# Three projections of a hybrid layer moved from one stage's fill to the next, and small and dense matrix products in a fixed turn

## The chip, the cores and the metric

The kernel runs on one core of one Trainium2 chip. The core has a matrix engine (TensorE, "PE" in the rows, with its weight loads as "PEld"), VectorE ("DVE"), ScalarE ("ACT"), GpSimd ("POOL") and SyncE ("SP"), whose queue issues the transfers. Each engine works through its own instructions in a fixed order and waits on semaphores for the others. The metric is the device time of one execution in microseconds, the median of several runs.

## What is computed

The reference is one inference step of two trunk layers. Each layer takes 384 tokens of width 1024 (128 of context, 256 latent), as a feed-forward half step, a mixer, and another feed-forward half step. The mixer is what matters here:

```python
def merge_branches(oa, ob, oc, zg, lp):
    ga, gb, gc = jnp.split(jax.nn.sigmoid(zg), 3, axis=-1)
    merged = ga * (oa @ lp['proj_a']) + gb * (ob @ lp['proj_b']) + gc * (oc @ lp['proj_c'])
    return merged @ lp['w_out']
```

`oa` and `ob` come from two kinds of attention with 8 heads each, `oc` from a recurrence with 8 heads of 64 that runs once in each direction, from projections r, k and v of the layer's input that pass a convolution over three tokens:

```python
def step(S, inp):
    r_t, w_t, k_t, v_t, kk_t, a_t = inp
    sa = jnp.einsum('bhvk,bhk->bhv', S, -kk_t)
    S = S * w_t[:, :, None, :] + sa[..., None] * (kk_t * a_t)[:, :, None, :] + v_t[..., None] * k_t[:, :, None, :]
    return S, jnp.einsum('bhvk,bhk->bhv', S, r_t)
```

## The kernel before

**Dense products.** All weights come as 128 x 128 blocks in one stream of 512 KB units of 8 blocks (`Stream`, line 370). Each unit is split by ScalarE into a rounded half `hi` and by VectorE into the rest, `lo` (both recorded at line 291, as nearly all instructions of these two engines). A chunk is one block times one slice of the input: three matmuls (lines 401, 402 and 403 in `mm3_steps`) of 128 x 128 by 384 columns. `mm3_steps` traces two chunks at a time, a block of 6 matmuls, and then yields a cost of 0.96 us (0.48 per chunk). A projection with its convolution is `conv_gen`: 8 chunks into the tile `pc`, an eviction by ScalarE and four VectorE instructions, and for a k the head norms (`kss`). Gates are written from `pz`, output projections from `pp`.

**The attention and its fill.** `attention` runs 8 pairs of heads through `heads_pair`, a chain of products (`sc`, `sl`), softmax on VectorE and ScalarE, transposes (`pt`) and output products (`po`). Between the steps of that chain it puts dense work from `front_fill`, which follows the plan `XP`: one string for each slot, in which g is a gate, n the next projection that the attention needs, p an output projection, and c the next projection for the recurrence out of the list `C_FIRST`. A slot spreads its string evenly over the steps of its pair. Dense work of a slot is put behind the attention's last matmul, so it does not run ahead of it.

**The recurrent stage.** `rwkv_gen` goes through four pairs of heads. For each, `rwkv_prepare` makes the inputs, `rwkv_chunks` turns the recurrence into products over chunks of 64 tokens, and `rwkv_scan` carries the state over. Pair 0's preparation comes first. After that the chunks of a pair are interleaved with the preparation of the next pair (`front`) and the scan of the pair before (`back`). In `rwkv_chunks` a long run of VectorE instructions ends in the tile `yr`; then come four groups of the smallest products, 48, 48, 24 and 24 calls of 16 or 32 rows by 32 weight columns, into the tile `pz` at line 1367 (the gates' `pz` stands at lines 401 to 403). Each call appears as two matmuls in the rows.

**What sets the order.** Matmuls of the recurrence go through `rmm`. After each, `beside` adds to a debt of dense work, in proportion to the product's size and to a rate (`RATES` by phase, `FR` outside), and takes blocks out of `mixer_fill` while the debt is positive. Yields of the generators add to the debt too: `RP` for each step of pair 0's preparation, `LAT` by phase, `RA` and `RS`. A scheduler then fixes the order of each engine with its own model of times, by priority. Each dense block is put behind the last product of the recurrence that was traced before it; nothing puts a product of the recurrence behind a dense block.

Of the kernel before, what the change touches and what calls it, by code (L numbers as in the profile page):

```python
# [32 lines left out]
OA = 50  # L33
SB = range(0,20)
SF = range(0,8,2)
FR = 0.3
PHASE = [0] * 4 + [1] * 3 + [2] * 4 + [3] * 10
RATES = (0.4, 0.2, 0.8, 0.3)
LAT = (0.2, 0.2, 0.0, 0.4)
RS = 2  # L40
RP = 7
OC = 100
PIL = 3
GAPS = (2, 1, 2, 0)
# [13 lines left out]
AHD = (4,)  # L58
HV = (3,)
AB = 6  # L60
XP = ('gggggg','nc','nggc','nc','nnnc','nnnpppppppp','nnn','nnnc','cc','c')
WY = (0.5, 0.5, 0.5, 1.5, 1, 1.5, 1, 1)
SCB = 2
LATE = 1
XS = 4
P3V = 0
PNV = 0
A0 = 4
A1 = 16
C_FIRST = ["tw", "al", "k0", "r0", "v0", "k1", "r1", "v1"]  # L70
CH = 64
NCH = NTOK // CH
NCC, NCL = NCTX // CH, NLAT // CH
# [223 lines left out]
def trunk(tc, I, O, order, taps=None, stop=None):  # L297
    nc = tc.nc
    PS = bass.MemoryType.PSUM
    es = ExitStack()  # L300
    V, S, G, T = Engine(nc.vector), Engine(nc.scalar), Engine(nc.gpsimd), nc.tensor
# [87 lines left out]
    def mm3(out, chunks, xs):  # L389

        n = len(chunks)
        for k, (w, x) in enumerate(zip(chunks, xs)):
            block3(out, w, x, k == 0, k == n - 1)

    def mm3_steps(out, chunks, xs, step=2):

        n = len(chunks)
        for k0 in range(0, n, step):
            for k in range(k0, min(n, k0 + step)):
                (wh, wl), (xh, xl) = chunks[k], xs[k]  # L400
                T.matmul(out, wh, xh, start=(k == 0), stop=False)  # L401
                T.matmul(out, wh, xl, start=False, stop=False)  # L402
                T.matmul(out, wl, xh, start=False, stop=(k == n - 1))  # L403
            if k < n - 1:
                yield 0.48 * step

# [6 lines left out]
    cc = cpool.tile([P, KD, 2], F32, name="cc")  # L413
# [18 lines left out]
    def vcol(l, name):  # L432
        o, n = VEC[name]
        return vecs[l][:, o : o + n]
# [500 lines left out]
    def gate_tile(keep):  # L935
        return keep.tile([P, NTOK], F32, tag="gate", bufs=2, name="gt")
# [14 lines left out]
    def front_fill(l, keep, pool, w, oa, need, head):  # L951

        conv = conv_gen(l, keep, pool, w, C_FIRST)
        todo = {"g": (1, (gate(l, 0, i, ax[i], head) for i in range(KD))), "p": (0.5, (project(l, "proj_a", i, ax[i], oa) for i in range(KD)))}
# [10 lines left out]

        for plan in XP:
            yield sum(todo[x][0] if x in todo else 1 for x in plan), some(plan)
# [6 lines left out]
    def mixer_fill(l, keep, pool, w, ob, gcd):  # L974

        for m in range(KD):
            if m == 0:
                yield from conv_gen(l, keep, pool, w, ["gl"])
            elif m in (2, 4):
                yield from conv_gen(l, keep, pool, w, [f"{n}{m // 2 + 1}" for n in "krv"])  # L980
            th = gate_tile(keep)
            yield from gate(l, 1, m, th)
            yield from project(l, "proj_b", m, th, ob)
        for m in range(KD):
            yield from gate_c(l, keep, m, gcd)
# [133 lines left out]
    def attention(l, pool, keep, w, oa, ob, head, spill):  # L1119
# [35 lines left out]
        debt = 0.0  # L1155
        for _ in range(XS):
            step(rest)
# [36 lines left out]
    def branch_a(l, pool, ready, soon, head):  # L1194
# [16 lines left out]
        nc.sync.dma_start(out=O["o_ka"][l], in_=kx[:, :NCTX])  # L1211
        soon.append([LATE, keys])
        yield 0.0
        yield from to_sbuf(l, A_V0, "pv", vx, head)
        nc.sync.dma_start(out=O["o_va"][l], in_=vx[:, :NCTX])
        soon.append([LATE, lambda: vt.append(token_major(pool, vx, "vt"))])
        yield 0.0
# [5 lines left out]
        for m in range(4):  # L1223
# [7 lines left out]

            soon.append([LATE, queries])
            yield 0.0

    def branch_b(l, pool, ready, soon):
# [3 lines left out]
        for m in range(4):  # L1239
# [26 lines left out]
            vt = []  # L1266
            soon.append([LATE, lambda vt=vt, vx=vx: vt.append(token_major(pool, vx, "vt"))])
            yield 0.96
# [16 lines left out]
    def conv_gen(l, keep, pool, w, names):  # L1285

        wsh = vcol(l, "w_shift")
        late = []
        for nm in names:
            i = C_INDEX[nm]  # L1290
            pz = mmp("pc")
            for n, cost in enumerate(mm3_steps(pz[:, :NTOK], stream.take("w_in", l, C_ORDER[i], KD), hs)):
                if n == 1 and late:
                    late.pop()()
                yield cost
            o = keep.tile([P, NTOK], F32, tag=("r" if nm[0] == "r" else nm), bufs=(2 if nm[0] == "r" else 1), name=nm)
            S.activation(out=o, in_=pz[:, :NTOK], func=AF.Copy, scale=wsh[:, 3 * i + 1 : 3 * i + 2])
            for a, b in STREAMS:
                V.scalar_tensor_tensor(out=o[:, a + 1 : b], in0=pz[:, a : b - 1], scalar=wsh[:, 3 * i : 3 * i + 1], in1=o[:, a + 1 : b], op0=ALU.mult, op1=ALU.add)
                V.scalar_tensor_tensor(out=o[:, a : b - 1], in0=pz[:, a + 1 : b], scalar=wsh[:, 3 * i + 2 : 3 * i + 3], in1=o[:, a : b - 1], op0=ALU.mult, op1=ALU.add)  # L1300
            w[nm] = o
            if nm == "tw":
                S.activation(out=o, in_=o, func=AF.Tanh)
            elif nm == "gl":
                S.activation(out=o, in_=o, func=AF.Tanh, scale=0.5)
                V.tensor_scalar(out=o, in0=o, scalar1=0.5, scalar2=0.5, op0=ALU.mult, op1=ALU.add)
            elif nm[0] == "k":

                p = int(nm[1])
                sq = gate_tile(keep)  # L1310
                S.activation(out=sq, in_=o, func=AF.Square, scale=vcol(l, "k_k")[:, p : p + 1])

                def norms(p=p, sq=sq):
                    pss = mmp("kss")
                    head_sums(pss, sq)
                    w[f"rn{p}"] = rn = keep.tile([P, 6], F32, name=f"rn{p}")
                    S.activation(out=rn, in_=pss[:, 0:6], func=AF.Sqrt)
                    V.tensor_scalar(out=rn, in0=rn, scalar1=1e-12, scalar2=None, op0=ALU.max)
                    V.reciprocal(rn, rn)

                late.append(norms)
            elif nm == "al":
                ka = keep.tile([P, 2, 4], F32, name="ka2")
                V.tensor_scalar(out=ka[:, 0], in0=vcol(l, "k_a"), scalar1=0.5, scalar2=None, op0=ALU.mult)
                V.tensor_scalar(out=ka[:, 1], in0=vcol(l, "k_a"), scalar1=-0.5, scalar2=1.0, op0=ALU.mult, op1=ALU.add)
                w["ka"] = ka
                hb = keep.tile([P, 2, 8], F32, name="hb")
                V.tensor_scalar(out=hb[:, 0], in0=vcol(l, "decay_w0"), scalar1=0.5, scalar2=None, op0=ALU.mult)
                V.tensor_scalar(out=hb[:, 1], in0=vcol(l, "iclr_a0"), scalar1=0.5, scalar2=None, op0=ALU.mult)
                w["hb"] = hb  # L1330
            yield 0.96
            yield 0.0
# [18 lines left out]
    rw_last = [None]  # L1351

    dense = [None, 0.0]
    rate = [FR]

# [8 lines left out]
            dense[1] -= b  # L1364

    def rmm(out, lhs, rhs, **k):
        rw_last[0] = T.matmul(out, lhs, rhs, **k)
        beside(lhs.shape[0], int(np.prod(lhs.shape[1:])), int(np.prod(rhs.shape[1:])))

    def rtr(out, src):  # L1370
# [27 lines left out]
    def rwkv_gen(l, pool, keep, w, oc, add):  # L1398
        gt = pool.tile([P, 2 * NU + 4, 3 * CH], F32, name="gt")

        end = gt[:, 2 * NU :].rearrange("p u x -> p (u x)")
        V.memset(end, 0.0)
        V.memset(end[:, 0:256:17], 1.0)
        t16 = end[:, 0:256].rearrange("p (a b) -> p a b", b=16)
        z1 = end[:, 256 : 256 + 32 * NU].rearrange("p (u t) -> p u t", t=32)
        fix = (gt, end, t16, z1)
        xs = [{} for _ in range(4)]
        for cost in rwkv_prepare(l, 0, w, pool, xs[0]):
            yield RP * cost
        for p in range(4):  # L1410
            back = ahead(rwkv_scan(l, p - 1, w, pool, keep, oc, xs[p - 1]), OC) if p else iter(())
            front = ahead(rwkv_prepare(l, p + 1, w, pool, xs[p + 1]), OA) if p < 3 else iter(())
            rate[0] = RATES[0]
            for i, cost in enumerate(ahead(rwkv_chunks(l, p, w, pool, fix, xs[p]), OB)):
                rate[0] = RATES[PHASE[i + 1]]
                yield LAT[PHASE[i]] * cost
                if i == 0:
                    add(0, f"v{min(p + 1, 3)}")
                if i in SB:
                    yield RA * next(back, 0)  # L1420
                if i in SF:
                    yield RA * next(front, 0)
            rate[0] = FR
            for b in chain(back, front):
                yield RA * b
        dense[1] = 0.0
        for cost in ahead(rwkv_scan(l, 3, w, pool, keep, oc, xs[3]), 500):
            yield RS * cost
# [326 lines left out]
    with es:  # L1755
        with tc.tile_pool(name="init", bufs=1) as pool:
# [15 lines left out]
            for c0 in range(0, KD, 2):  # L1772

                offset = 9000 - 1000 * c0
                i, cols = c0 // 4, slice(256 * (c0 % 4), 256 * (c0 % 4) + 512)
                pa = rwp("ada")
                for k in range(0, KD, 2):
                    w = pool.tile([P, 2, 512], F32, tag="adaw", bufs=KD, name="adaw")
# [60 lines left out]
```

## Time and profile before

| what | value |
| --- | --- |
| runs | 2411.74, 2412.66, 2422.63 us; median 2412.66 |
| profiled execution | 2413.25 us, span 2411.4 us, mean granted clock 0.985 |
| instructions in the span | 42684 |
| TensorE busy | 2289.0 us |
| VectorE busy | 1689.8 us |
| ScalarE busy | 1066.2 us |
| GpSimd busy | 409.2 us |

The span runs from the first to the last instruction. Matmuls overlap in the engine, so the distance between two starts, and not a matmul's own duration, tells what it takes. A wait in the timeline is given in brackets behind the instruction that it precedes, with what ended it.

### The profile page before, as it was taken

How to read it: one execution, taken by the hardware profiler on the slowest of the kernel's cores; microseconds unless marked ns; L12 is line 12 of the kernel's file. 1: busy time of each engine (PE TensorE's matmuls, PEld its weight loads, DVE VectorE, ACT ScalarE, POOL GpSimd, SP SyncE). 2: the span in 40 equal slices, each digit the busy share in tenths (PEclk: the TensorE clock that was granted, in tenths of full speed). 3: DMA queues.
4: the chain of work that ended last, by engine and by line, in shares of the span. 5: the costliest groups of instructions: out<-in, count | busy, mean ns of one | idle time of the engine just before them, and what ended most of it. 6: DMA issues, size and time to landing. Idle time of an engine off the chain costs nothing.

```text
span 2411.4 us, 42684 instructions
## 1 busy us (share of the span) xinstructions
PE 2289.0 (95%) x17066; PEld 2098.1 (87%) x17066; DVE 1689.8 (70%) x2949; ACT 1066.2 (44%) x1962; POOL 409.2 (17%) x426
## 2 busy tenths in 40 slices
PE   8999899998899999999899999999989999999998
PEld 6999888887777788999889999888877777899997
DVE  3896877767767567876879964767787674775534
ACT  3333245655545445433243332556555454453322
POOL 1000421001122034000430003300022220530003
PEclk9999999999899999999999999999999999999999
DMA  8775544242111262665546733533321112634332
GB/s 307 246 244 184 184 115 124 90 116 71 37 61 48 72 212 88 218 205 178 168 148 218 246 127 126 153 95 93 112 71 33 55 54 81 216 122 132 123 125 85
DMA packets 125078, 324.53 MB, mean 135 GB/s; under 512 B 31568, under 2 KB 50256, under 8 KB 124880
## 3 DMA queue, kind: packets, MB, share of 16 engines
q1 hardware_dynamic: 124880, 321.81, 41.6%
q8 instruction: 134, 2.20, 0.4%
q14 instruction: 64, 0.52, 0.1%
HBM read 312.06 MB, written 9.70 MB: 133 GB/s over the span
## 4 chain that ended last, share of the span: by engine, by line
PE 74%; DVE 12%; ACT 5%; issue 3%; POOL 3%; DMA 1%; SPq 0%; ACTq 0%; POOLq 0%; DVEq 0%
PE po L403 5%; PE po L402 5%; PE po L401 5%; PE pa L385 4%; PE pa L386 4%; PE pg L385 4%; PE pg L386 4%; PE pa L387 4%; PE pg L387 4%; DVE lo L291 3%; ACT hi L291 2%; PE pz L401 2%; PE pz L402 2%; PE pz L403 2%; POOL ax L291 1%
## 5 line engine op out<-in xcount | busy, mean ns | idle before, releaser
L291 ACT ACTIVATE hi<-raw 128x1024 fp32r<-128x1024 f32 x418 | 441.7, 1058 | 743.1 <-issue 227.1
L291 DVE TENSOR_TENSOR lo<-raw,hi 128x1024 fp32r<-128x1024 f32 (+1 forms) x472 | 551.4, 1177 | 303.3 <-ACT hi L291 301.0
L291 DVE SCALAR_TENSOR_TENSOR acc<-adaw,cs,acc 128x1024 f32<-128x1024 f32 x224 | 289.0, 1330 | 0.0
L403 PE MATMUL po<-uh,lo 128*128 128x384 f32 x704 | 238.3, 338 | 10.7 <-DVE lo L291 10.5
L401 PE MATMUL po<-uh,hi 128*128 128x384 f32 x704 | 238.7, 339 | 0.0
L402 PE MATMUL po<-ul,hi 128*128 128x384 f32 x704 | 237.5, 337 | 0.0
L385 PE MATMUL pa<-zh,hi 128*128 128x384 f32 x584 | 198.7, 340 | 0.0
L386 PE MATMUL pa<-zl,hi 128*128 128x384 f32 x584 | 197.4, 338 | 0.0
L385 PE MATMUL pg<-zh,hi 128*128 128x384 f32 x584 | 197.2, 338 | 0.0
L387 PE MATMUL pa<-zh,lo 128*128 128x384 f32 x584 | 196.3, 336 | 0.6 <-DVE lo L291 0.6
L386 PE MATMUL pg<-zl,hi 128*128 128x384 f32 x584 | 196.6, 337 | 0.0
L387 PE MATMUL pg<-zh,lo 128*128 128x384 f32 x584 | 196.2, 336 | 0.0
L291 POOL TENSOR_TENSOR sa<-ax,ax 128x384 f32<-128x384 f32 x12 | 15.8, 1312 | 788.8 <-DVE ax L291 585.2
L403 PEld LDWEIGHTS po<-uh,lo 128*128 128x128 f32 x704 | 133.2, 189 | 13.2 <-DVE lo L291 13.2
L401 PE MATMUL pz<-zh,hi 128*128 128x384 f32 x352 | 127.0, 361 | 8.3 <-ACT hi L291 2.8
L401 PEld LDWEIGHTS po<-uh,hi 128*128 128x128 f32 x704 | 133.0, 189 | 2.1 <-issue 1.5
L402 PEld LDWEIGHTS po<-ul,hi 128*128 128x128 f32 x704 | 133.0, 189 | 0.5
L403 PE MATMUL pz<-zh,lo 128*128 128x384 f32 x352 | 124.8, 355 | 2.2 <-DVE lo L291 2.2
L402 PE MATMUL pz<-zl,hi 128*128 128x384 f32 x352 | 123.8, 352 | 0.0
L385 PEld LDWEIGHTS pa<-zh,hi 128*128 128x128 f32 x584 | 109.6, 188 | 4.9 <-ACT hi L291 3.7
L387 PEld LDWEIGHTS pa<-zh,lo 128*128 128x128 f32 x584 | 110.1, 189 | 0.9 <-DVE lo L291 0.9
L387 PEld LDWEIGHTS pg<-zh,lo 128*128 128x128 f32 x584 | 110.1, 189 | 0.0
(398 smaller groups left out, 5323.5 us busy)
## 6 DMA issues: line engine op xcount, KB each, us to landing
raw<-ws SPq DMA_DIRECT2D x418, 512.0 KB, 3.5
adaw<-wada SPq DMA_DIRECT2D x144, 512.0 KB, 4.5
bm<-rpb SPq DMA_DIRECT2D x64, 64.0 KB, 7.9
axd<-ax SPq DMA_DIRECT2D x16, 192.0 KB, 4.2
gcd<-gt SPq DMA_DIRECT2D x16, 192.0 KB, 4.6
gc<-gcd SPq DMA_DIRECT2D x16, 192.0 KB, 3.4
ax<-axd SPq DMA_DIRECT2D x16, 192.0 KB, 4.7
xt<-xt SPq DMA_DIRECT2D x8, 192.0 KB, 8.4
```

The costliest lines, as they stand in the source:

```text
L291: self.last = f(*a, **k)
L385: T.matmul(out, wh, xh, start=first, stop=False)
L386: T.matmul(out, wh, xl, start=False, stop=False)
L387: return T.matmul(out, wl, xh, start=False, stop=last)
L401: T.matmul(out, wh, xh, start=(k == 0), stop=False)
L402: T.matmul(out, wh, xl, start=False, stop=False)
L403: T.matmul(out, wl, xh, start=False, stop=(k == n - 1))
```

## The change

The list of projections in the attention's fill ends after those of pair 0. k1, r1 and v1 are taken at the start of the recurrent stage's fill, ahead of `gl`. The plan of the attention's slots has one c less in its third, seventh and eighth slot (the first string fills the time before the loop). The rates of the debt change, the preparation's factor goes from 7 to 5, and 2 us are added once, for pair 0, at the yield in front of the smallest products. `mm3_steps` notes the last matmul of each block in `filled`; `rmm` puts a product with up to 32 weight columns behind that matmul, when there was a block since the last product of the recurrence.

```diff
-FR = 0.3
+FR = 0.35
 PHASE = [0] * 4 + [1] * 3 + [2] * 4 + [3] * 10
-RATES = (0.4, 0.2, 0.8, 0.3)
+RATES = (0.5, 0.25, 0.7, 0.35)
...
-RP = 7
+RP = 5
...
-XP = ('gggggg','nc','nggc','nc','nnnc','nnnpppppppp','nnn','nnnc','cc','c')
+XP = ('gggggg','nc','nggc','n','nnnc','nnnpppppppp','nnn','nnn','c','c')
...
+FIRST = 2
...
-C_FIRST = ["tw", "al", "k0", "r0", "v0", "k1", "r1", "v1"]
+C_FIRST = ["tw", "al", "k0", "r0", "v0"]
...
+    filled = [None]
+
     def mm3_steps(out, chunks, xs, step=2):
...
                 T.matmul(out, wh, xl, start=False, stop=False)
-                T.matmul(out, wl, xh, start=False, stop=(k == n - 1))
+                filled[0] = T.matmul(out, wl, xh, start=False, stop=(k == n - 1))
...
             if m == 0:
-                yield from conv_gen(l, keep, pool, w, ["gl"])
+                yield from conv_gen(l, keep, pool, w, ["k1", "r1", "v1", "gl"])
...
     def rmm(out, lhs, rhs, **k):
-        rw_last[0] = T.matmul(out, lhs, rhs, **k)
+        small = int(np.prod(lhs.shape[1:])) <= 32
+
+        with tc.issue_after(filled[0].ins) if small and filled[0] is not None else ExitStack():
+            rw_last[0] = T.matmul(out, lhs, rhs, **k)
+        filled[0] = None
         beside(lhs.shape[0], int(np.prod(lhs.shape[1:])), int(np.prod(rhs.shape[1:])))
...
-                yield LAT[PHASE[i]] * cost
+
+                yield LAT[PHASE[i]] * cost + (FIRST if p == 0 and i == 6 else 0)
```

## Rows read from the trace of the kernel before

**Rows 1.** The page, busy time, share and instructions of the engines.

```profile
PE 2289.0 (95%) x17066; PEld 2098.1 (87%) x17066; DVE 1689.8 (70%) x2949; ACT 1066.2 (44%) x1962; POOL 409.2 (17%) x426
```

**Rows 2.** Busy time by stretch: attention, recurrent stage, first layer, then second.

```profile
core 0: us, PE busy (x) PEld busy (x) DVE busy (x) ACT busy (x) POOL busy (x), PEclk, DMA share, GB/s
378.00:563.50 185.50, 179.82 (x1058) 160.49 (x1060) 127.81 (x336) 108.86 (x272) 3.10 (x3) 0.99 0.33 96
563.50:862.50 299.00, 277.05 (x3483) 227.64 (x3479) 207.14 (x435) 148.10 (x275) 60.30 (x90) 0.97 0.18 58
1570.00:1756.70 186.70, 179.60 (x1060) 160.26 (x1062) 129.02 (x339) 110.23 (x276) 3.09 (x3) 0.99 0.33 97
1756.70:2051.00 294.30, 272.31 (x3481) 224.37 (x3477) 207.62 (x435) 148.05 (x276) 61.05 (x90) 0.98 0.19 59
```

**Rows 3.** Timeline of TensorE at the joints between pairs of the attention.

```profile
436.98 0.45 PE L1069 MATMUL sl<-kh,qs 128*128 128x384 f32 x1 [0.66 <-ACT pe L291]
...
518.64 0.86 PE L1097 MATMUL po<-ptl,vt 128*64 128x256 f32 x5 [1.38 <-ACT ptl L291]
...
539.89 0.44 PE L401 MATMUL pc<-zh,hi 128*128 128x384 f32 x1
...
560.78 0.65 PE L1097 MATMUL po<-ptl,vt 128*64 128x256 f32 x2 [1.82 <-ACT ptl L291]
...
562.87 1.54 PE L1097 MATMUL po<-ptl,vt 128*64 128x256 f32 x5 [0.64 <-ACT ptl L291]
```

**Rows 4.** Timeline of TensorE around the first pair's smallest products.

```profile
611.05 0.34 PE L402 MATMUL pc<-zl,hi 128*128 128x384 f32 x1
611.23 0.33 PE L403 MATMUL pc<-zh,lo 128*128 128x384 f32 x1
...
614.62 0.98 PE L1367 MATMUL pz<-yr,gt 16*32 16x16 f32 x96 [2.41 <-DVE yr L291]
615.53 0.44 PE L401 MATMUL pc<-zh,hi 128*128 128x384 f32 x1
615.81 0.34 PE L402 MATMUL pc<-zl,hi 128*128 128x384 f32 x1
...
620.24 0.52 PE L403 MATMUL pc<-zh,lo 128*128 128x384 f32 x1
620.56 0.52 PE L401 MATMUL pc<-zh,hi 128*128 128x384 f32 x1
```

**Rows 5.** Waits of TensorE by releaser in 563.5 to 862.5: total, times, longest.

```profile
PE pz L1367 <- DVE yr L291: 3.0, 2, 2.4
...
PE pz L403 <- DVE lo L291: 1.1, 1, 1.1
...
PE pp L401 <- ACT hi L291: 0.6, 1, 0.6
```

**Rows 6.** VectorE: two groups of the attention; then busy times of the run-up.

```profile
L291 DVE TENSOR_TENSOR lo<-raw,hi 128x1024 fp32r<-128x1024 f32 (+1 forms) x30 | 35.6, 1188 | 25.2 <-ACT hi L291 25.1
...
L291 DVE SCALAR_TENSOR_TENSOR k<-pc,vec,k 128x127 f32<-128x127 f32 (+1 forms) x8 | 3.2, 407 | 0.0
...
563.50:614.60 51.10, 45.15 (x293) 37.69 (x290) 42.87 (x77) 24.46 (x44) 13.06 (x22) 0.98 0.20 64
```

**Rows 7.** Line 402 alone, a third of all dense matmuls, in two stretches.

```profile
563.50:614.60 51.10, 17.15 (x50) 9.47 (x50) 0.98 0.20 64
614.60:628.00 13.40, 3.28 (x6) 1.76 (x6) 0.62 0.13 44
```

**Rows 8.** Three stretches at a lower clock; of the second, tile `pc` alone.

```profile
614.60:628.00 13.40, 12.97 (x304) 11.00 (x306) 7.77 (x19) 5.82 (x10) 0.00 (x0) 0.62 0.13 44
1808.00:1816.00 8.00, 3.61 (x11) 2.47 (x10) 0.41 (x1) 0.00 (x0) 0.57 0.02 5
748.00:754.00 6.00, 5.09 (x27) 4.66 (x28) 4.11 (x7) 2.17 (x5) 1.66 (x3) 0.72 0.25 90
```

## The prediction

> **What bounds the kernel now.** I read the page first: TensorE is busy for 95% of the span [rows 1], so work that is only moved from one place to another on this engine can gain nothing but TensorE's waits, a lower clock, or the cost of changing between kinds of product. Then I cut the span into the two stages that the change touches, in both layers [rows 2]. The attention, with its fill, takes 185.5 us in the first layer and 186.7 in the second, and TensorE waits for 5.7 and 7.1 us of them: it is bound by TensorE. The recurrent stage takes 299.0 and 294.3 us with 22.0 us of waits in each, and its mean granted clock is 0.97 and 0.98. What there is to gain lies in the second stage: some 22 us per layer of waits, and stretches at half clock. The last two views say where. The timeline of TensorE [rows 3, 4] shows the waits between the attention's pairs and in front of the smallest products; the waits by releaser [rows 5] show that none but those for `yr` (3.0 us), the input of the first group of smallest products, is large.
>
> **Part 1: 24 chunks leave the attention.** k1, r1 and v1 are three projections of 8 chunks, 3 matmuls each: 72 matmuls. Dense ones start 0.175 us apart in a run (611.05, 611.23) [rows 4], so TensorE loses 72 x 0.175 = 12.6 us of work per layer here. The attention's chain of pairs does not get shorter by itself, so waits appear where the removed projection was the cover. Slots lose one projection each: the third ("nc" to "n"), the seventh ("nnnc" to "nnn") and the eighth ("cc" to "c"). The trace has both forms of the joint: after a slot "nnn" TensorE waits 1.38 us at 518.64, after the slot "nnnc" a `pc` matmul starts at 539.89 with no wait [rows 3]. I add 1.4 us each for the third and the seventh (the third waits 0.66 us already, at 436.98), and 0.5 us for the tail, whose 1.82 and 0.64 us of waits [rows 3] stand behind a chain that also loses the convolutions' work on VectorE. That is 3.3 us of new waits; the bounds are none, and the whole 12.6 us (each slot as long as before). Attention: -12.6 + 3.3 = -9.3 us per layer.
>
> **Part 2: they come into the recurrent stage.** +12.6 us of TensorE work per layer. With them move 3 weight transfers of 512 KB; DMA stands at 0.18 there against 0.33 in the attention [rows 2], so these are hidden behind the stage, on SP's queue too. On VectorE move 12 convolution steps of 0.41 us and 3 `lo` halves of 1.19 us [rows 6], 8.5 us, and on ScalarE the 3 `hi` halves and evictions; ScalarE is busy for half of the stage [rows 2] and hides them.
>
> **Part 3: the run-up to the first small product.** From 563.5 to 614.6 the first pair's chain goes through VectorE, which is busy for 42.9 of 51.1 us [rows 6], and TensorE waits 51.1 - 45.15 = 5.95 us, the 2.41 us before the first small product included [rows 4, 6]. 50 matmuls of each of the three dense kinds, 150 in all, ran by then [rows 7]. More had been released, but it stood behind the small products in TensorE's fixed order. Now the first small product has to come after all dense work released before it. By the constants that is 4 x 5 us in the preparation, some 8 us more in the chunks and 2 us of FIRST: 30 us at 0.48 per chunk, 62 chunks or 186 matmuls, to which the attention's leftover of 12 comes in either version. So 186 + 12 - 150 = 48 more matmuls run before that point: 8.4 us. VectorE gets the 8.5 us of part 2 in the same run-up and has 8.2 us free; I take half of it as added to the chain, 4.2 us. Then the waits are 5.95 + 4.2 - 8.4 = 1.7 us: 4.2 us gained. Bounds: nothing (VectorE's work all lengthens the chain) and 5.95. The gain is real only if the work done early is not missing as cover later. At the end of the stage the dense work still stands between the last scan's steps, and by the constants some 14 chunks stay for it: enough, I take it.
>
> **Part 4: turns.** The 144 calls of the smallest products per pair cost 0.055 x 0.7 each: 5.5 us of dense work, six blocks of 6 matmuls. The added edge names what is queued: the small product behind a block waits for its last matmul, and everything of the recurrence behind that small product waits too, ScalarE's eviction of the group after it. If the block's weights are late, the recurrence is late; that is a rival below. What changing costs: from the small products at 614.62 into dense work the first dense matmul takes 0.28 us to the next one's start (615.53 to 615.81), 0.105 more than in a run [rows 4]; with the same on the way out, 0.2 us a turn. Four of the six blocks fall between groups, where dense matmuls stand already; two per pair split a group. 2 x 4 x 0.2 = 1.6 us per layer; bounds none and 24 x 0.2 = 4.8.
> The Trainium skill has a rule against this: TensorEngine Tiling (Array Packing), Tiling Modes, says that a change of the tiling mode, not just of the tile, drains the engine. By that rule, the trace agrees that a change costs, with 0.105 us [rows 4]; should it cost a whole dense matmul, the sum would be rival 4's.
>
> **Part 5: the clock.** From 614.6 to 628 the mean granted clock is 0.62 [rows 8]: it falls to the lower of its two levels, 1.2 GHz, after the wait of 2.41 us and the small groups, and dense matmuls start 0.32 us apart (620.24, 620.56) [rows 4]. 18 dense matmuls ran there [rows 7]: 18 x (0.32 - 0.175) = 2.6 us lost. In the second layer 11 ran from 1808 to 1816 at a clock of 0.57 [rows 8]: 1.6 us. With the wait filled and dense work inside the groups I take both as regained; the bounds are none of it, and besides these the fall at 748 to 754 (0.72 [rows 8]: slow for 3.4 us, some 10 matmuls, 1.5 us), which comes with another pair and which I leave.
>
> **Sum.** First layer: -9.3 + 12.6 - 4.2 + 1.6 - 2.6 = -1.9 us. Second: -9.3 + 12.6 - 4.2 + 1.6 - 1.6 = -0.9. Together -2.8. The profiled execution took 2413.25 us (span 2411.4, and 1.85 around it), 0.6 over the median of the runs: 2413.25 - 2.8 = 2410 us. The change moves 25 us of TensorE's work and gives back little of it.
>
> **Rivals.**
> 1. The stage swallows the moved work: of the waits left there, 22.0 - 4.2 = 17.8 us per layer, half goes as well, since dense work is released faster (rates 0.5, 0.25 and 0.35), and the fall at 748 too. 2410 - 2 x 8.9 - 1.5 = 2391 us. For it: the waits are many and small, and dense work is always at hand. Against it: most of them lie before larger products (`scan`, `pg`), in an order that the change does not touch. Chance 0.36.
> 2. The other side: a forced block waits for its weights. TensorE goes in order, and where a dense matmul waits for `lo` or `hi` it does so for 1.1 and 0.6 us now [rows 5]; VectorE, which makes `lo`, is the busy one before the small groups [rows 6]. If half of the 24 blocks per layer wait 0.85 us, that is 10.2 us per layer, and such waits leave the clock low (2.6 and 1.6 us not regained): 2410 + 20.4 + 4.2 = 2435 us. It decides from 0.32 us per block on (24 x 2 x 0.32 = 15 us, past half a per cent). Against it: such waits are two of the stage's many now. Chance 0.13.
> 3. The attention gives back less: a wait of 2.6 us at each of three joints in place of 3.3 in all, 4.5 more per layer: 2419 us, still within half a per cent. Chance 0.09.
> 4. Each change of mode empties the engine, priced by a dense matmul's own 0.34 us each way [rows 4]: 24 turns x 0.68 = 16.3 us per layer in place of 1.6: 2410 + 29 = 2439 us. The row's 0.105 us speaks against this price [rows 4]. Chance 0.05. The Trainium skill, TensorEngine Tiling (Array Packing), Tiling Modes, has the engine drained at each change of mode, which would speak for it.
>
> **How the numbers follow.** The forecast has 0.37, the largest. Half a per cent, 12 us, is about what a measurement of this kernel can tell from no change. Within it (2401 to 2425) are the forecast and rival 3: 0.46. Faster: rival 1, 0.36. Slower: rivals 2 and 4, 0.18. The likeliest case alone reaches from 2400 to 2422 (clock not regained and 3 us more of turns per layer; or no new waits in the attention and the run-up's whole 5.95 us). The 8-in-10 range takes in rival 1 and the nearer half of rival 2: 2384 to 2430 us.
>
> **What would show it.** Attention: 72 fewer dense matmuls per layer, its stretch shorter by about 9 us, waits of 1 to 3 us at the third and the seventh joint. Run-up: no wait before the first `pz`, and about 48 more dense matmuls by then. Small groups: a block of 6 dense matmuls inside the first two, 0.28 us at each change, and no 0.32 us spacing behind them. Stage: longer by about 7 us. The prediction is wrong if the stage grows by less than 2 us (rival 1) or if TensorE waits for `lo` or `hi` in front of blocks for more than 8 us per layer (rival 2).

## The result: slower, and the stage's profile after

The changed kernel takes 2624.67 us (median of four runs, 2620.38 to 2636.33); the kernel before, on the same chip, 2414.12. The ratio is 1.0873, interval 1.0829 to 1.0917: slower by 8.7%, some 210 us, where 2410 us was forecast. It lies far outside the range. The profiled execution's span is 2622.5 us.

The page's line of engines, to be held against [rows 1]:

```profile
PE 2424.8 (92%) x17066; PEld 2177.5 (83%) x17066; DVE 1699.0 (65%) x2955; ACT 1070.2 (41%) x1962; POOL 414.4 (16%) x426
```

TensorE has the same 17066 instructions and is busy for 136 us more. A matmul that runs at the lower clock counts as busy for longer (0.52 us in place of 0.34 in [rows 4]), so this is no more work. The windows of the attention and the recurrent stage, first layer, then second (columns as in [rows 2]):

```profile
371.00:560.50 189.50, 176.46 (x1019) 154.64 (x1019) 129.05 (x340) 109.86 (x280) 2.60 (x4) 0.97 0.32 92
560.50:963.50 403.00, 354.68 (x3510) 279.12 (x3509) 213.86 (x438) 157.11 (x284) 64.53 (x90) 0.82 0.14 47
1674.00:1860.50 186.50, 172.61 (x1019) 151.66 (x1019) 128.92 (x340) 109.63 (x280) 2.46 (x4) 1.00 0.33 97
1860.50:2250.00 389.50, 337.93 (x3505) 266.47 (x3505) 214.10 (x437) 156.47 (x283) 63.96 (x90) 0.87 0.15 48
```

The whole loss is in the recurrent stage: 403.0 and 389.5 us, where [rows 2] have 299.0 and 294.3. (The windows do not begin and end at the same instructions before and after, so 189.5 and 185.5 us do not compare the attention's length. Between the starts of the attention's last `po` and of the stage's last `gss` the stage takes 410.6 and 397.5 us instead of 292.7 and 288.9.) VectorE, ScalarE and GpSimd do nearly the same work there as before and are less busy in proportion. The mean granted clock is 0.82 and 0.87 instead of 0.97 and 0.98. Between its two levels, 0.82 means that TensorE stood at 1.2 GHz for 0.36 of the stretch, some 145 us; before, 0.97 meant some 18.

Where the chain is held, VectorE's timeline tells first: these two lines write `yr`, the operand of the first group of smallest products, for the first and the second pair.

```profile
612.84 1.09 DVE L292 STREAM_TRANSPOSE yr<-ty 128x512 f32<-128x512 f32 x1
...
729.21 1.12 DVE L292 STREAM_TRANSPOSE yr<-ty 128x512 f32<-128x512 f32 x1 [0.16 <-ACT ty L292]
```

And TensorE's timeline, at the attention's joints and then around these two points:

```profile
436.11 0.70 PE L1114 MATMUL rope<-qx,ca 128*128 128x256 f32 x2 [1.90 <-ACT qx L292]
...
518.96 0.44 PE L1100 MATMUL po<-ptl,vt 128*64 128x256 f32 x2 [1.38 <-ACT ptl L292]
...
540.93 0.44 PE L1100 MATMUL po<-ptl,vt 128*64 128x256 f32 x2 [1.38 <-ACT ptl L292]
...
618.45 0.92 PE L1373 MATMUL up<-tw,wl 64*128 64x384 f32 x4
...
631.28 0.69 PE L404 MATMUL pc<-zh,hi 128*128 128x384 f32 x1 [4.07 <-ACT gt L292]
...
638.18 1.65 PE L1373 MATMUL bon<-bo,con 128*128 128x384 f32 x2 [2.69 <-POOL bo L292]
639.62 1.49 PE L1373 MATMUL gg<-gl,gu 128*128 128x384 f32 x2
640.34 1.09 PE L404 MATMUL pc<-zh,hi 128*128 128x384 f32 x1
...
642.51 0.52 PE L406 MATMUL pc<-zh,lo 128*128 128x384 f32 x1
642.96 0.51 PE L1373 MATMUL pz<-yr,gt 16*32 16x16 f32 x20
...
742.70 1.65 PE L1373 MATMUL bon<-bo,con 128*128 128x384 f32 x2 [7.35 <-POOL bo L292]
744.14 1.49 PE L1373 MATMUL gg<-gl,gu 128*128 128x384 f32 x2
...
747.11 0.43 PE L1373 MATMUL pz<-yr,gt 16*32 16x16 f32 x30
```

`yr` is ready at 613.9, and the first small product starts at 642.96, 29.0 us later. In [rows 4] TensorE waited for `yr` and started at once. What it does meanwhile is dense work, and the preparation of the next pair (`up`, `bon`) with the waits of that: 2.69 us for GpSimd's `bo`. A dense matmul waits 4.07 us for ScalarE's `gt`, the eviction of a gate. Right ahead of the small product stands one block of six dense matmuls (640.34 to 642.51). The second pair is ready at 730.3 and starts at 747.1, behind the next pair's `bon`, which itself waits 7.35 us. Added over the four pairs of the first layer, from the end of `yr<-ty` to the first small product, the small products are held for 29.0 + 16.8 + 25.7 + 3.7 = 75.2 us. Before the change the same sum is 1.8 us. The Trainium skill, TensorE: Matmul & The Clock Gate, Step-by-step: what each phase is for, says that matmuls stay in program order and only weight loads are pulled ahead; the trace agrees, with these 29.0 us for which a ready product stands behind others.

The waits of TensorE in the first layer's stage, 560.5 to 963.5 (columns as in [rows 5]):

```profile
PE bon L1373 <- POOL bo L292: 10.0, 2, 7.3
PE pz L1373 <- DVE yr L292: 5.4, 4, 2.2
PE scan L1373 <- DVE sp L292: 4.5, 3, 2.6
PE p L1373 <- ACT xt L292: 4.2, 4, 2.5
PE pc L404 <- ACT gt L292: 4.1, 1, 4.1
```

The largest is a wait of the next pair's preparation, which before had time to spare. What it costs the chain is more than it shows, because the ready small products stand behind it.

The 48 `p` products of the first pair, by tile (columns: window, its length, busy time of these products, clock, DMA share, GB/s) and in TensorE's timeline, before and then after:

```profile
629.00:640.00 11.00, 3.10 (x48) 0.89 0.07 22
...
629.51 3.10 PE L1367 MATMUL p<-atq,xt 64*64 64x128 f32 x48
```

```profile
661.00:692.00 31.00, 9.92 (x48) 0.50 0.05 17
...
661.79 2.82 PE L1373 MATMUL p<-atq,xt 64*64 64x128 f32 x18 [0.58 <-ACT xt L292]
664.54 0.69 PE L404 MATMUL pz<-zh,hi 128*128 128x384 f32 x1
665.16 1.11 PE L1373 MATMUL p<-atq,xt 64*64 64x128 f32 x4
...
674.58 0.42 PE L1373 MATMUL p<-atq,xt 64*64 64x128 f32 x1
```

They follow the small groups directly and depend on them. Before, they run in one piece and are through in 3.1 us; after, they run at 1.2 GHz throughout, with six single dense matmuls between them, and take 13.2 us, from 661.79 to 675.00.

Where the time went can be put together as an estimate for the first layer, whose window grows by 104 us. TensorE's waits in it go from 299.00 - 277.05 = 22.0 to 403.00 - 354.68 = 48.3 us, 26 more. At half clock pass 142 us in place of 18 (the table below); dense matmuls start 0.32 us apart there and not 0.175 [rows 4], so that 0.45 of these 124 us, or 56, is lost. The moved work is 12.6 us at full speed. That is 95 of 104.

### The profile page after: what moved, and what is told of

Its sections match the earlier page's. It is cut to its first block, busy times and chain, and to the rows that moved or that the text cites. A ratio compares the mean times of both kernels' runs of the same rounds, so it can differ in the third digit from the quotient of the medians.

```text
span 2622.5 us, 42662 instructions
## 1 busy us (share of the span) xinstructions
PE 2424.8 (92%) x17066; PEld 2177.5 (83%) x17066; DVE 1699.0 (65%) x2955; ACT 1070.2 (41%) x1962; POOL 414.4 (16%) x426
## 5 line engine op out<-in xcount | busy, mean ns | idle before, releaser
L404 PE MATMUL pz<-zh,hi 128*128 128x384 f32 x352 | 142.0, 403 | 9.2 <-DVE kx L292 2.6
L406 PEld LDWEIGHTS po<-uh,lo 128*128 128x128 f32 x704 | 133.2, 189 | 13.2 <-DVE lo L292 13.2
L405 PE MATMUL pz<-zl,hi 128*128 128x384 f32 x352 | 134.0, 381 | 0.0
L406 PE MATMUL pz<-zh,lo 128*128 128x384 f32 x352 | 132.3, 376 | 0.9 <-DVE lo L292 0.9
L292 DVE TENSOR_TENSOR mt<-pm,con 128x128 f32<-128x128 f32 (+1 forms) x32 | 11.3, 354 | 158.2 <-PE pm L1373 158.2
```

Source lines behind the costliest of these rows:

```text
L292: self.last = f(*a, **k)
L406: filled[0] = T.matmul(out, wl, xh, start=False, stop=(k == n - 1))
```

## Experiments

Theory and rivals, as they developed: the added order does the harm (A) or the new rates do (B) or the late projections starve the stage (C); then, for the order, the turns (T) or what a small product waits behind (D, L, I, B of the last runs); for the move, its amount (A of those runs), its place (P, Q) or VectorE's steps (V). Each time is set against the kernel before on the same chip (medians 2411.3 to 2416.7). "Held" is the sum made above and "half clock" the time at 1.2 GHz from the attention's end (the start of its last `po`) to the last `gss`, both in us in the first layer; "dense first" counts the dense matmuls between the attention's end and the first small product.

| kernel | us | ratio, interval | held | half clock | dense first |
|---|---|---|---|---|---|
| before | 2414 | | 1.8 | 18 | 150 |
| changed | 2624.67 | 1.0829 to 1.0917 | 75.2 | 142 | 222 |
| order alone | 2588.22 | 1.0661 to 1.0756 | 59.6 | 115 | 252 |
| move + constants | 2476.35 | 1.0224 to 1.0271 | 5.5 | 50 | 168 |
| move alone | 2498.99 | 1.0317 to 1.0372 | 1.5 | 73 | 166 |
| order + move | 2623.94 | 1.0833 to 1.0882 | 57.9 | 131 | 252 |
| constants alone | 2446.14 | 1.0081 to 1.0135 | 0.6 | 14 | 133 |

**The parts, one and two at a time.** The order alone is the diff's `filled` and `issue_after` lines on the kernel before; the move alone is its `XP`, `C_FIRST` and `conv_gen` lines.

> The kernel before with the new edge alone: a small product comes behind the last dense matmul traced before it; projections, plan and rates as before. Theory A (the edge does the harm: it ties the recurrence to low-priority dense work): at least half of the loss of 210 us, 2520 to 2620 us, with waits before the smallest products and granted clock below 0.96. Theory B (too much dense work released at the wrong time by the new rates): 2405 to 2425 us. Theory C (the late projections starve the recurrent stage): 2405 to 2425 us.

> The changed kernel without the new edge: projections moved, plan and rates new. Theory A: within 1% of the kernel before, 2395 to 2430 us; this would be the prediction's own sum without its part on turns. Theory B: most of the loss stays, above 2500 us. Theory C: above 2500 us.

> The kernel before with the projections moved and the plan of the slots new, but the old rates and no edge. Theory A: 2395 to 2430 us, near the run without the edge. Theory B: 2405 to 2425 us. Theory C: above 2500 us.

> Edge and moved projections with the old rates, and without the 2 us before the first small products. Theory A: as slow as the changed kernel or slower, 2560 to 2680 us, since the old factor of 7 in the preparation leaves more dense work that the first small product has to wait for. Theory B: 2405 to 2425 us. Theory C: above 2500 us, no faster than the run with the move alone.

The order costs 173 us by itself and the move 84; together they cost 209, so they overlap. The constants take 23 us off the move and nothing off order and move together. A is right on the two kernels with the order and wrong on the two without it. That the move by itself costs 84 us only C came near to (above 2500 us, measured 2498.99), but C is wrong on the order alone and 24 us out on move + constants. Adding the order to move + constants costs 148 us, 74 per layer, and the held time rises by 75.2 - 5.5 = 69.7 us in the first layer: nearly the same amount. That they come out so close is in part luck. On the kernel before, the order costs 87 us per layer for 59.6 - 1.8 = 57.8 us more held; the rest goes with the half clock, 115 us in place of 18.

**The constants on the kernel before.**

> The kernel before with the new constants alone (rates, FR, RP, FIRST), no move and no added order. The constants took 23 us off the move (2499 to 2476). If they are better in themselves: 2390 to 2410. If they only make room for the moved work and here exhaust the dense work early: 2415 to 2450, and TensorE's clock falls late in the stage.

They cost 29 us (ratio 1.0108), as the second case had it, but its reason holds for one layer only: half clock is 14 and 38 us in the two layers, where it was 18 and 10. Why they cost so much is not settled.

**The order: where the wait is.** One kernel gives priority to the dense products traced between recurrent ones, one keeps the order only between two small products (`hot` is the priority offset of the matmuls in `mm3_steps`):

```
 def beside(k, m, n):
...
+                hot[0] = OB
                 b = next(dense[0], None)
+                hot[0] = 0
```

```
-        with tc.issue_after(...) if small and filled[0] is not None ...
+        with tc.issue_after(...) if small and was[0] and filled[0] is not None ...
...
+        filled[0], was[0] = None, small
```

> The kernel before with the added order alone, and the dense matmuls that are traced between recurrent products given the chunk chain's own priority offset (200) instead of none. Theory D (a small product has to wait in the fixed order for a dense block of lower priority, and the next pair's preparation and the previous pair's scan are placed ahead of that block): the harm of the order alone (2588) goes nearly away, 2405 to 2470, first small product of layer 0 at about +50 us after the attention. Theory T (the turns themselves cost: emptying the array, slower products): stays at 2540 to 2640.

> The kernel before with the added order only between two small products: the first small product after any other recurrent product does not wait for dense work traced before it. Theory D with the wait at the first product of a group: the first group comes at about +50 us again and the time falls to 2420 to 2500. Theory T, or theory D with waits inside the groups: 2550 to 2600, as with the whole added order (2588).

With priority: 2537.04 us (1.0473 to 1.0536), a gain of 51 us on the order alone, but nearer to T. The held time hardly moves (57.0); half clock falls from 115 to 85, and `p` products and dense matmuls no longer alternate. Inside groups only: 2595.44 (1.0699 to 1.0758), no better than the whole order. TensorE's timeline of that run shows why:

```profile
613.02 0.39 PE L1372 MATMUL pz<-yr,gt 16*32 16x16 f32 x26 [2.43 <-DVE yr L291]
...
616.05 0.91 PE L1372 MATMUL up<-tw,wl 64*128 64x384 f32 x2 [1.06 <-DVE v L291]
...
639.58 1.54 PE L1372 MATMUL bon<-bo,con 128*128 128x384 f32 x2 [1.88 <-POOL bo L291]
...
642.20 1.28 PE L1372 MATMUL gg<-gl,gu 128*128 128x384 f32 x2
...
645.66 0.51 PE L1372 MATMUL pz<-yr,gt 16*32 16x16 f32 x39
```

The group starts at once, as before, and stops after 26 of its products: the next one stands behind a dense block, and by that block's time about 100 dense matmuls, `up`, `bon` and `gg` have run. It is the same hold, now 32 us between two products of one group.

**The order with less dense work ahead, and with both remedies.** `RP = 7` becomes `RP = 3` in the first, second and fourth of these kernels; the second has the priority of above for the products too, and the third and the fourth trace the whole block (`with tc.issue_after(...), tc.high_priority(offset=OB):`), evictions and weights with it, at the chain's priority.

> The added order alone with RP 3 in place of 7: so much less dense work is traced ahead of the first pair that, in the fixed order, about 150 dense matmuls stand before the first small product of a layer, as in the kernel before, and not 252. Theory L (the order costs because a small product must now let all dense work go first that was traced before it: the recurrence loses its lead, and later runs without dense work): first small product back at about +50 us, 2430 to 2510. Theory T (the turns): 2550 to 2600, as the order alone (2588).

> The added order alone with both remedies: RP 3 (150 dense matmuls ahead of the first small product, not 252) and the chunk chain's priority for the dense matmuls that are traced between recurrent products. Theory D+L (a small product must wait for the dense blocks traced before it, and those wait behind the next pair's preparation, which the fixed order puts first; each remedy alone leaves the other wait): first small product back at +48 to +56 us, the 8.4 and 7.1 us waits of the next pair's bon gone, 2415 to 2480. Theory T (the turns or something else in the order): 2530 to 2620.

> The added order alone, with everything a dense block between recurrent products issues (weights, products, and the evictions on ScalarE and VectorE that free its PSUM buffer) at the chunk chain's priority, not the products alone. Theory I (the dense block that a small product waits for is held through its eviction and buffers by work that goes ahead of it): the small products are held for under 25 us per layer, where the order alone holds them 60, and 2430 to 2500. Theory B (it is the number of dense matmuls traced before it): held about 57 us as in the run with priority for the products alone, 2520 to 2560.

> As the run with whole blocks at the chain's priority, with RP 3 in place of 7. Theory I: little more than it or less, 2415 to 2500. Theory B: the count falls and with it the wait, but the evictions do not matter: 2560 to 2600, as with priority for the products alone and RP 3 (2598).

RP 3: 2619.41 (1.0815 to 1.0871), a miss for L and above T's range too. Both remedies: 2597.7 (1.073 to 1.0788), a miss for D and L together, in the range of T, which reads there "the turns or something else in the order". Whole blocks: 2554.47 (1.0543 to 1.0591), in B's range; with RP 3, 2605.08 (1.0768 to 1.0813), 5 us above it. They hold the small products for 76.2, 74.3, 60.0 and 72.0 us, so I falls. The priority in these kernels reaches only the blocks that `beside` takes after a product. Those that the yields release, through `add` with the same `issue_after(rw_last[0].ins)`, keep the old one, and they include the dense work of the preparation ahead of the first pair; so what a priority for all blocks would do is not shown. With RP 3 exactly 150 dense matmuls run before the first small product, as before, and it still comes late. TensorE's timeline of RP 3 alone, where `yr` is ready at 614.2:

```profile
629.93 1.65 PE L1372 MATMUL bon<-bo,con 128*128 128x384 f32 x2 [8.41 <-POOL bo L291]
...
632.51 1.63 PE L1372 MATMUL gg<-gl,gu 128*128 128x384 f32 x2
...
635.99 0.40 PE L1372 MATMUL pz<-yr,gt 16*32 16x16 f32 x12
```

Of 21.8 us, 8.4 are TensorE's wait for the next pair's `bo`. So it is not the dense work alone that stands ahead. The code gives the link, and it was there before the change:

```
    def beside(k, m, n):
...
            with tc.issue_after(rw_last[0].ins):
                b = next(dense[0], None)
```

A dense block is ordered behind the recurrent product traced last, of whatever pair: the next pair's `bon`, the previous pair's `scan`. The new line orders a small product behind a dense block. Together they order it behind the product that the recurrence traced last before that block, and TensorE then waits for GpSimd, VectorE and ScalarE on behalf of other pairs. For the first group that product is set by a constant: with `SF = range(0,8,2)` the fourth step of the next pair's preparation, which ends in `bon`, is traced at i = 6, directly ahead of the step with these products. A priority for the dense block does not take the order away. The traces agree: in the changed kernel's first and second pair and in RP 3's first, `bon` and `gg` are followed by one block of six dense matmuls and then by the small product. And without the order, the second pair's `bon` runs well after the first pair's first small product (650.75 against 614.62 before the change, 635 against 613.63 with move and constants), and with it, ahead (638.18 against 642.96 in the changed kernel, and in the fence above). This is read from the code and the order of the instructions; a kernel whose dense blocks are ordered behind products of their own pair only, which would take away this link and leave the rest, was not tried.

> The whole change (order, move, new constants), and the chunk chain's priority for the dense matmuls traced between recurrent products. Theory D: the order's part of the loss shrinks as it did without the move (2588 to 2537), so 2550 to 2590 where the change takes 2625. If it is the move that makes the order wait: 2610 to 2640.

> Control: the kernel before with dense blocks at the chain's priority and without the added order. If the priority is harmless in itself, 2405 to 2440; if dense work at the chain's priority holds up the chain by itself, over 2460, and the two runs above carry that much.

The changed kernel with priority takes 2589.5 (1.0686 to 1.0756), at the upper edge of D's range; held 56.5. The control takes 2431.26 (1.0051 to 1.0082): the priority itself costs 18 us. It holds the small products for 17.7 us in the first layer, behind dense work alone, and costs 9 us per layer: a hold that only brings dense work forward costs less than its length.

**The move: VectorE, amount or place.**

> The move alone (old constants, no added order), with the 12 shift steps on VectorE left out for k1, r1 and v1 in each layer (the token shift of these three is not computed). Theory V (the moved projections' VectorE steps stand in the recurrent chain's way, and the chain's steps in theirs): 2410 to 2445 where the move with them takes 2499. Theory S (it is the moved products' place in the dense supply, not VectorE): 2480 to 2500.

> The move alone, with the products of three of branch c's eight gates (72 dense matmuls in each layer; their weights are still fetched) left out, so that the recurrent stage has as many dense matmuls as before. Theory A (the stage has no room for more dense work: the amount is what costs): the 42 us that the stage grew by per layer go away nearly whole, 2390 to 2430. Theory P (k1, r1 and v1 stand at the head of the stage's dense order, all other dense work behind them, and the chain waits or runs without dense work): 2450 to 2490.

> The kernel before, with three of branch c's eight gates multiplied twice in each layer: 72 more dense matmuls late in the stage, no other change. Theory A: 12.6 us per layer at full clock, up to the 42 that the move cost, so 2440 to 2495. Theory P: hidden or appended at full speed, 2415 to 2442.

> Only v1 moves (24 dense matmuls in each layer, 8.4 us in both at 0.175), no added order, old constants. In proportion to the move of all three (84 us): 2440 to 2450. If the stage takes a third of the work into its gaps and the attention's 3 us per layer are kept: 2405 to 2420.

> The move alone, with k1, r1 and v1 one step later in the stage's dense order: behind gl, the first gate and the first projection of branch b instead of ahead of them. Amount as in the move (2499), another place. Theory P (at the head of the order they keep the gates from standing beside the first pairs' small products): 2450 to 2485. Theory Q (the next pair waits for v1, so later is worse): 2510 to 2560. Neither: 2490 to 2508, and the place within the stage hardly matters.

Edits: `for a, b in STREAMS if nm[1] != "1" else ():` in `conv_gen`; `if m in (2, 4, 6): stream.take(...)` without its products in `gate_c`; the products of the same three gates run twice on the kernel before; `"v1"` alone in the stage; and `elif m == 1:` for the three projections in `mixer_fill`.

Without the shifts 2494.05 (1.0293 to 1.0343), against 2498.99 with them: VectorE's steps are not it, V falls. With the old amount 2466.41 (1.0181 to 1.0232): of the 84 us, 33 go and 50 stay, which is P's range and not A's. The same amount added late to the kernel before costs 37 us (2453.68, 1.0118 to 1.0185), which is A's range and not P's. So the amount is worth 33 to 37 us, 16 to 19 per layer, where full speed would be 12.6, and none of it is hidden. All three projections one step later, behind `gl` and the first gate: 2500.48 (1.0331 to 1.0391), no difference, so P in its form (the head of the order) and Q fall. v1 alone: 2436.26 (1.0053 to 1.0109), 20 us, between its two cases. Windows from the attention's end to the last `gss` in the run with the old amount, both layers:

```profile
562.90:868.90 306.00, 276.51 (x3397) 228.75 (x3396) 203.69 (x442) 148.92 (x273) 61.72 (x88) 0.90 0.15 49
1778.60:2083.60 305.00, 275.75 (x3396) 227.67 (x3395) 203.24 (x442) 148.92 (x273) 61.65 (x88) 0.90 0.15 50
```

The clock is 0.90, where [rows 2] have 0.97 and 0.98. Two stretches of the move alone, at its third pair, and the 34.4 us behind its last `gss`, show what goes with the move:

```profile
744.00:757.00 13.00, 9.60 (x244) 7.75 (x243) 8.51 (x20) 5.43 (x11) 0.00 (x0) 0.64 0.25 84
757.00:765.00 8.00, 8.00 (x36) 6.14 (x35) 0.00 (x0) 0.94 (x1) 0.00 (x0) 0.52 0.00 0
...
866.60:901.00 34.40, 32.24 (x180) 31.02 (x181) 11.09 (x18) 13.34 (x19) 3.37 (x3) 1.00 0.80 266
```

From 744 to 752 only 3 dense matmuls run beside 192 small products; the clock falls, and from 757 to 765 TensorE is busy all the time at 0.52. The recurrence ends 10 us later than before in this layer (303.1 us after the attention in place of 292.7), but the dense work has fallen behind: 34.4 us of it (`pz` and `pp`, 0.80 DMA share) run alone at the end, where before 2 us did. The waits ahead of this name the dense stream itself:

```profile
PE kss L1337 <- ACT gt L291: 7.6, 3, 5.7
...
PE pc L401 <- ACT gt L291: 2.1, 1, 2.1
```

Per layer the remaining 25 us can be put together from the trace of the old-amount run: 8 us more of TensorE's waits in the stage, some 45 us more at half clock in the first layer, each worth (0.320 - 0.175) / 0.320 = 0.45 us of dense work, or 20 us, less 5 us of shorter attention: 23. That is an account and not a test; no run changed the clock alone, and why the dense stream is not beside the small products after the move stays open.

## Why the prediction was wrong

**What bounds the kernel** held: TensorE does, and work that is only moved gains nothing but waits and clock. The prediction took this as a bound on gains and hardly as a risk. With the one-sided order TensorE had 22 us of waits per layer and 18 and 10 us of half clock; both were small, and both could grow.

**Part 1, the attention,** was right. From the first `sc` to the last `po` it takes 189.4 and 186.6 us instead of 196.3 and 195.8, which is 8.1 us less on average (forecast 9.3). New waits are 4.4 us per layer (forecast 3.3); in the first layer 1.2 and 1.4 of them stand at 436.11 and 540.93, the third and the seventh joint, as said.

**Part 2, the amount,** was mis-sized: 12.6 us per layer, measured 16 to 19 (the two runs on amount). The shifts on VectorE are worth 2.5 us per layer at most (5 us in both, with intervals that overlap). That the moved projections also leave the small products without dense work beside them, some 25 us per layer, was no term of the sum.

**Part 3, the run-up,** had the direction of the count right and its value wrong. Forecast: 48 more dense matmuls before the first small product, no wait in front of it. Measured: 222 - 150 = 72 more, and no wait in front of it. But the product comes 82.5 us after the attention and not 49.6. The waits saved there were to be a gain of 4.2 us; the row shows TensorE without a wait because the ready product stands behind others. The sentence "More had been released, but it stood behind the small products in TensorE's fixed order" named the lead that the recurrence had, and the sum took it away for nothing.

**Part 4, the turns,** is the step that failed. Its price was right: in the changed kernel at full clock a dense matmul is followed by a small product after 0.27 us (42 cases) and a small product by a dense one after 0.11 (35), against 0.175 and 0.01 in runs, 0.2 us for a pair of changes. In the two layers there are 54 such entries where there were 44: 2 us in all. The Trainium skill, TensorEngine Tiling (Array Packing), Tiling Modes, has the engine drained at a change of mode; the trace agrees that a change costs, at 0.2 us the pair. What the part left out is what stands ahead of the dense block. It said that a small product "waits for its last matmul" and looked behind the block only; ahead of it stand the dense blocks traced earlier and the recurrent products of other pairs. The sum had no term for it. It is a hold of 70 us in the first layer, where the order costs 74 per layer.

**Part 5, the clock,** went the other way: half clock from 18 to 142 us in the first layer and from 10 to 98 in the second, not regained. Dense work spent early is missing later, which Part 3 had named as its condition ("enough, I take it").

**The rivals.** Rival 2 had the right side and the wrong place: no wait for `lo` or `hi` is among the stage's larger ones, and its 0.85 us per block is far below the measured hold. Rival 1's ground, dense work always at hand, is what the move itself undoes. Rivals 3 and 4 did not happen.

## What to carry to other kernels

Before an order is added between two kinds of work on one engine, follow it backwards through the orders that are there already: if A goes behind B and B behind the last C, A now waits for C, whoever C belongs to. A priority given to some of B did not lift that here (57 to 74 us held). Look in the trace of before at the lead that the waiting chain has (how much of the other work, traced earlier, runs later, and which products of other pairs), and not only at the cost of a switch. The count of dense matmuls alone is no price: with RP 3 it was 150 as before, and the product was still held for 21.8 us. And a stage whose dense work ends with its chain has no room: here what was moved in was paid with 33 to 37 us where full speed would be 25, and the move cost another 50 us, which were not traced to one cause.

## What was not expected of the hardware

TensorE was busy without a gap while its clock stood almost all the time at 1.2 GHz: 8.00 of 8.00 us at 0.52 in the move alone. And a change between dense matmuls and products of 16 or 32 rows by 32 columns is cheap, 0.2 us for the pair, with 54 of them in the changed kernel.
